# Layer 0's first projection in the order v, RG-LRU, k, q, S5, gates; S5 tables on VectorE held until k is evacuated; S5's end states written later

## The chip, the core and the metric

The kernel runs on one core of a Trainium2 chip. TensorE (PE) multiplies matrices into PSUM, VectorE (DVE), ScalarE (ACT) and GpSimd (POOL) do the elementwise work, and SyncE (SP) issues the DMAs. The metric is the device time of one execution in microseconds.

## The reference, cut to what matters

Two layers run over a prompt of 512 frames and eight running streams of 16 frames each. A layer adds to x the output projection of three mixers side by side, then a squared-ReLU MLP:

```python
hn = _rms_norm(x, p['norm1'])
proj = hn @ p['w_in']                       # u_a, g_a, u_b, q, k, v
out_a = rglru(u_a, g_a)                     # conv of 4, gates, scan, times gelu(g_a)
out_b = s5(u_b)                             # complex scan; z = gelu(y + d*u); z * sigmoid(z @ w_glu + b_glu)
out_c = window_attention(rope(q), rope(k), v, sinks)
x = x + concat(out_a, out_b, out_c) @ w_out
x = x + square(relu(_rms_norm(x, p['norm2']) @ w_up)) @ w_down
```

The outputs are x after both layers and a last norm, and the new states: the last three inputs of the convolution, the last RG-LRU state, the last complex S5 state, and the last keys and values. S5's discretised matrices (A, B, C and powers of A) are computed from the weights inside the kernel.

## The kernel before, in words

All is float32. The 640 columns (512 prompt and 128 sample frames) are cut into two groups g = 0 and 1 of 256 prompt and 64 sample columns, so a matmul moves 320 columns. Activations lie with features on the partitions.

Each projection is a list of `Unit`s. A unit makes 128 output features of one group: 8 slices of 128 input features, in two halves of 4, into one of three PSUM banks of the tag `mm`. `stream` runs units and yields after each half. In the first layer's `in_proj` the weights are used as float32 (line 271, operands `raw` for the first half of a unit and `wl` for the second). Other units split their weights into a high part on ACT (L243, `wh<-raw`) and a rest on DVE (L244, `wl<-raw,wh`), and then take three matmuls for each slice (L274 to L276).

`in_proj` has 12 units: `ua` and `ub` (two each, inputs of RG-LRU and S5), `k`, `v`, four `q`, and two gates `ga`. Their numbers 0 to 11 are in this order, and a unit's output has to be read out of its bank (evacuated) before the third unit after it can start. Evacuations multiply by the norm's factor r: `v` by one DVE operation (L692); `k` and `q` by four ACT copies to `sw` (L705, L706), a POOL product with sin*r (L707) and DVE products with cos*r (L716 for k, L710 for q); `ua` and `ub` of layer 0, group 0, by ACT copies that need no r (L675, L676, L670), with the product by r on POOL later. r comes from the squares (ACT L382, POOL L389, with one buffer `sq` between them, and a last sum on DVE, L386), from sums on PE (L395), a reciprocal root on DVE (L414 to L421), a broadcast on PE (L432) and a copy on ACT (L434). `cs` holds the rope's cos and sin; POOL multiplies both by r (L741).

The first layer's set-up runs at the same time: `s5_small` (DVE operations of 128x32, lines 450 to 536) makes A and its factors, and `layer_small` starts `s5_const`, whose complex products `cmul` (lines 541 to 547, 128x256 each) make the B tables on DVE and the C tables on POOL.

After the first units come the mixers. `mixers` yields after each step of RG-LRU, S5 and attention, and `weave` puts halves of the stream F (the rest of this `in_proj`, then the other group's) between them. The order on PE is the order of the program. The orders on ACT, DVE, POOL and SP are made by a list scheduler, with a model of the time and priorities (`high_priority` for evacuations), so that an edit in one place can move instructions in others. Every engine runs its own list in order. The main program is:

```python
turns(A, 2)
...
small = layer_small(0, P)
next(small)
first(1)
turns(A, 10)
M = mixers(0, P, 0, q[0], m[0], setup[0])
F = chain(A, stream(in_proj(0, 1, norms[1], q[1])))
weave(M, tw[0:9], F, 9)
run(small)
weave(M, tw[9:], F, 19)
```

`first(1)` loads x of group 1 and issues its squares. The mixers of group 1 follow, woven with what is left of F, the output projection of group 0 and its MLP.

Of the kernel before, what the change touches and what calls it, by code (L numbers as in the profile page):

```python
# [11 lines left out]
F32 = mybir.dt.float32  # L12
# [135 lines left out]
def encoder_kernel(ctx: ExitStack, tc: tile.TileContext, a, o):  # L148
# [516 lines left out]
    def in_evac(L, P, g, q, kind, i, pt):  # L665
        r = q.r
        in_alloc(q, *{"ua": ("uap",), "k": ("kS",), "v": ("vS",), "q": ("q", "qS")}.get(kind, (kind,)))
        early = q.early[kind] if kind in q.early else 0
        if kind == "ub" and i < early:
            act(q.ub[:, i], pt, AF.Copy)  # L670
            G.tensor_tensor(q.ub[:, i], q.ub[:, i], r, OP.mult)
        elif kind == "ua" and i < early:
            u = q.uap[:, i]
            v = u[:, 259:335].rearrange("p (b t) -> p b t", t=19)[:, :, 3:19]
            act(u[:, 3:259], pt[:, 0:256], AF.Copy)  # L675
            act(v, pt[:, 256:320].rearrange("p (b t) -> p b t", t=16), AF.Copy)  # L676
            G.tensor_tensor(u[:, 3:259], u[:, 3:259], r[:, 0:256], OP.mult)
            G.tensor_tensor(v, v, r[:, 256:320].rearrange("p (b t) -> p b t", t=16), OP.mult)
        elif kind == "ua":
            u = q.uap[:, i]  # L680
            tt(u[:, 3:259], pt[:, 0:256], r[:, 0:256], OP.mult)
            tt(u[:, 259:335].rearrange("p (b t) -> p b t", t=19)[:, :, 3:19],
               pt[:, 256:320].rearrange("p (b t) -> p b t", t=16), r[:, 256:320].rearrange("p (b t) -> p b t", t=16), OP.mult)
        elif kind == "ub":
            tt(q.ub[:, i], pt, r, OP.mult)
        elif kind == "ga":
            t = tp.tile([128, NG], F32, tag="t", name="t", bufs=2)
            tt(t, pt, r, OP.mult)
            gelu2(V, q.ga[:, i], t)
        elif kind == "v":  # L690
            vT = tp.tile([128, NG], F32, tag="t", name="t", bufs=2)
            tt(vT, pt, r, OP.mult)  # L692
            gcopy(q.vS, vT[:, 256:320])

            def turn():
                b = bank3("sm", 2, 128)
                for j in range(2):
                    transpose(b[:, j], vT[:, 128 * j:128 * j + 128])
                act(kvs[L]["vt"][:, 2 * g:2 * g + 2], b, AF.Copy)

            return turn
        else:
            sw = tp.tile([128, NG], F32, tag="sw", name="sw", bufs=2)
            for p in range(0, 128, 64):
                act(sw[p:p + 32], pt[p + 32:p + 64], AF.Copy)  # L705
                act(sw[p + 32:p + 64], pt[p:p + 32], AF.Copy)  # L706
            G.tensor_tensor(sw, sw, q.sinr, OP.mult)  # L707
            if kind == "q":
                t = tp.tile([128, NG], F32, tag="t", name="t", bufs=2)
                tt(t, pt, q.cosr, OP.mult)  # L710
                tt(q.q[:, i], t[:, 0:256], sw[:, 0:256], OP.add)
                v4 = lambda z: z[:, 256:320].rearrange("p (b t) -> p b t", t=16)
                tt(q.qS[:, :, i], v4(t), v4(sw), OP.add)
            else:
                t = tp.tile([128, NG], F32, tag="t", name="t", bufs=2)
                tt(t, pt, q.cosr, OP.mult)  # L716
                tt(kvs[L]["kT"][:, 256 * g:256 * g + 256], t[:, 0:256], sw[:, 0:256], OP.add)
                tt(q.kS, t[:, 256:320], sw[:, 256:320], OP.add)

    kvs = {}  # L720

    def in_proj(L, g, norm, q, raws=None):

        w_in = a["w_in"][L]
        units = [("ua", 0), ("ua", 1), ("ub", 0), ("ub", 1), ("k", 0), ("v", 0)]
        units += [("q", i) for i in range(4)] + [("ga", 0), ("ga", 1)]
        order = (4, 5, 6, 7, 8, 9, 0, 1, 2, 3, 10, 11) if L == 0 and g == 0 else range(12)

        def begin():
            if g == 0:  # L730
                kvs[L] = {"kT": cst.tile([128, 512], F32, tag="kT", name="kT"), "vt": cst.tile([128, 4, 128], F32, tag="vt", name="vt")}
            q.early = {"ua": 2, "ub": 2} if L == 0 and g == 0 else {"ua": 2}

        def factors():
            norm.finish()
            q.r = norm.r
            cs = tp.tile([128, 2, NG], F32, tag="cs", name="cs", bufs=1)
            q.cosr, q.sinr = cs[:, 0], cs[:, 1]
            dma(cs, a["rope"][g])
            for t in (q.cosr, q.sinr):  # L740
                G.tensor_tensor(t, t, q.r, OP.mult)  # L741

        def evac(kind, i):
            def f(pt):
                with tc.high_priority():
                    return in_evac(L, None, g, q, kind, i, pt)

            return f

        items = [Unit(w_in[n], [(lambda: norm.h, evac(*units[n]))], norm, norm.full, raws if n == order[0] else None) for n in order]  # L750
        items[1].mid, items[2].mid = norm.flush, factors
        return [begin] + items
# [59 lines left out]
    def s5(L, P, g, q, mix, c):  # L812
# [69 lines left out]
        for ct, gs in cts:  # L882
# [5 lines left out]
            n4 = lambda t: t.rearrange("p (n t) -> p n t", t=4)  # L888
            V.scalar_tensor_tensor(n4(zz[:, ct]), n4(u[:, ct]), col("ssm_d", 2 * L + ct), b.rearrange("p t n -> p n t"), OP.mult, OP.add)
            gelu2(V, zz[:, ct], zz[:, ct])  # L890

        sl = D[:, :, 63:80:4]
        for h in range(2):
# [5 lines left out]
        G.tensor_tensor(e, e, bl, OP.add)  # L899
        gcopy(P["send"][:, 128:144], e[:, :, 0])  # L900
        gcopy(P["send"][:, 64 * g:64 * g + 64].rearrange("p (b g) -> p g b", b=4), e[:, :, 1:5])
        sg = c.at(1280, 2, NG)
        yield
        for ct in range(2):
            b = bank("sm")[:, 0:NG]
            for k in range(2):
                mm(b, lhsT=P["wglu"][:, k, 128 * ct:128 * ct + 128], rhs=zz[:, k], start=k == 0, stop=k == 1)  # L907
            act(sg[:, ct], b, AF.Tanh, scale=0.25, bias=hcols[:, 8 + 2 * L + ct:9 + 2 * L + ct])
        V.scalar_tensor_tensor(sg, sg, 1.0, zz, OP.add, OP.mult)
        mix = mix()  # L910
        act(mix[:, 2:4, 0], sg, AF.Copy, scale=0.25)
        V.scalar_tensor_tensor(mix[:, 2:4, 1], sg, 0.25, mix[:, 2:4, 0].bitcast(F32), OP.mult, OP.subtract)
        if g == 1:
            dma(o["send"][L], P["send"])

# [212 lines left out]
        evac = lambda k: lambda pt: out_tile(L, g, k, pt, hm[g])  # L1128
        return [begin] + [Unit(a["w_out"][L, k], [(lambda: mix["mix"](0), evac(k))]) for k in range(8)]

    mark = {}

    def up_evac(norm, am, f, pt):
        t = tp.tile([128, NG], F32, tag="t", name="t", bufs=2)
        V.scalar_tensor_tensor(t, pt, 0.0, norm.r, OP.max, OP.mult)  # L1135
# [33 lines left out]
    def first(g):  # L1169
        norms[g] = Norm(g, n1(0), full=True)  # L1170
        raws = []
        for k in range(0, 8, 2):
            dma(xT[:, g, k:k + 2], a["x"][g, :, k:k + 2])
            if g == 0 and k < 4:
                raws.append(wload(a["w_in"][0, 4], k // 2))
        for k in range(8):
            norms[g].add(k)
        return raws
# [28 lines left out]
    small_prep()  # L1207
    s5_small(lru_const())
    small = layer_small(0, P)
    next(small)  # L1210
    first(1)
    turns(A, 10)
    M = mixers(0, P, 0, q[0], m[0], setup[0])
    tw = WEIGHTS[True]
    F = chain(A, stream(in_proj(0, 1, norms[1], q[1])))
# [72 lines left out]
```

## Time and profile before

| quantity | value |
|---|---|
| median of 3 runs | 1442.09 us (1441.71 to 1443.01) |
| profiled execution, its own time | 1444.44 us |
| its span, first to last instruction | 1442.7 us |
| PE busy | 1384.6 us, 96% |
| DVE, ACT, POOL busy | 857.1, 631.6, 355.5 us |
| PE busy from 330 to 700 us | 368.96 of 370 us |
| PE busy from 190 to 250 us | 52.26 of 60 us |

PE is busy nearly all the time, so the time is the sum of its work, of the waits on PE, and of the stretches in which its granted clock was at the lower of its two levels. A busy share of another engine says little by itself: what counts is whether PE waited for it.

### The profile page before, as it was taken

What the parts mean: (1) busy time and instruction counts of PE and PEld (TensorE: products, weight loads), DVE (VectorE), ACT (ScalarE), POOL (GpSimd) and SP (SyncE); (2) the same over time, 40 slices, a digit from 0 to 9 for tenths busy, and PEclk for the clock granted to TensorE, in tenths of its full rate; (3) what the DMA queues carried; (4) which work ended last, traced back from release to release, by engine and by line L of the source; (5) the groups of instructions that cost most, each with busy time, mean ns of one, the idle gap of its engine ahead of it and who ended that gap; (6) DMA issues with size and microseconds to landing.
All of it is one profiled execution on the core that took longest, in us unless ns stands there. A gap on an engine that the chain in (4) does not pass through costs nothing.

```text
span 1442.7 us, 25209 instructions
## 1 busy us (share of the span) xinstructions
PE 1384.6 (96%) x9390; PEld 1303.2 (90%) x9390; DVE 857.1 (59%) x1702; ACT 631.6 (44%) x1315; POOL 355.5 (25%) x575
## 2 busy tenths in 40 slices
PE   8897989999999999999989998999999999999997
PEld 6565678899999999999988897889999999999997
DVE  7677278766644344446687768775664434434574
ACT  3344475545432123135675667654543312313543
POOL 4546053601014007001244225420100100100111
PEclk8899999999999999999989999999999999999998
DMA  6221223244422222234423342333442222223452
GB/s 236 77 78 65 87 90 127 89 159 142 152 90 80 75 74 67 78 108 149 132 91 105 112 148 75 125 105 118 147 147 95 74 80 75 80 75 109 148 176 95
DMA packets 91387, 156.24 MB, mean 108 GB/s; under 512 B 14336, under 2 KB 18304, under 8 KB 91264
## 3 DMA queue, kind: packets, MB, share of 16 engines
q1 hardware_dynamic: 91264, 154.63, 32.2%
q8 instruction: 74, 1.21, 0.3%
q14 instruction: 49, 0.40, 0.1%
HBM read 151.02 MB, written 3.37 MB: 107 GB/s over the span
## 4 chain that ended last, share of the span: by engine, by line
PE 80%; DVE 6%; POOL 5%; ACT 3%; issue 2%; DVEq 0%; POOLq 0%; ACTq 0%
PE mm L274 24%; PE mm L276 23%; PE mm L275 23%; PE mm L271 3%; PE sm L176 1%; PE sm L1045 1%; DVE wl L244 1%; DVE bigf L861 1%; PE sm L1024 1%; PE sm L879 1%; PE sm L907 1%; PE fin L432 1%; DVE bigf L864 0%; DVE bigf L866 0%; PE fin L395 0%
## 5 line engine op out<-in xcount | busy, mean ns | idle before, releaser
L276 PE MATMUL mm<-bigr,wl 128*128 128x320 f32 x2496 | 777.4, 311 | 18.4 <-DVE wl L244 18.4
L274 PE MATMUL mm<-bigr,wh 128*128 128x320 f32 x2496 | 785.5, 315 | 2.4 <-POOL bigr L156 1.9
L275 PE MATMUL mm<-bigr,wh 128*128 128x320 f32 x2496 | 775.2, 311 | 1.7 <-DVE bigr L1138 1.6
L243 ACT ACTIVATE wh<-raw 128x512 fp32r<-128x512 f32 x496 | 312.0, 631 | 482.8 <-PE mm L275 462.7
L276 PEld LDWEIGHTS mm<-bigr,wl 128*128 128x128 f32 x2496 | 472.2, 189 | 23.1 <-DVE wl L244 22.5
L274 PEld LDWEIGHTS mm<-bigr,wh 128*128 128x128 f32 x2496 | 472.3, 189 | 13.5 <-issue 6.8
L275 PEld LDWEIGHTS mm<-bigr,wh 128*128 128x128 f32 x2496 | 472.6, 189 | 3.0 <-DVE bigr L1138 2.4
L244 DVE TENSOR_TENSOR wl<-raw,wh 128x512 fp32r<-128x512 f32 x496 | 352.9, 712 | 171.4 <-ACT wh L243 161.2
L156 POOL TENSOR_SCALAR bigr<-t 128x320 fp32r<-128x320 f32 x128 | 61.9, 485 | 613.2 <-ACT t L1136 612.5
L1120 DVE TENSOR_TENSOR xT<-xT,mm 128x320 f32<-128x320 f32 x160 | 77.8, 486 | 128.4 <-PE mm L276 128.0
L1138 DVE TENSOR_TENSOR bigr<-t,bigr 128x320 fp32r<-128x320 f32 x128 | 70.6, 551 | 73.4 <-POOL bigr L156 73.3
L1136 ACT ACTIVATE t<-t 128x320 f32<-128x320 f32 x128 | 60.1, 472 | 122.3 <-DVE t L1135 103.0
L1135 DVE SCALAR_TENSOR_TENSOR t<-mm,r 128x320 f32<-128x320 f32 x128 | 62.3, 489 | 77.0 <-PE mm L276 76.3
L389 POOL TENSOR_TENSOR ss<-ss,sq 128x320 f32<-128x320 f32 x52 | 50.9, 979 | 202.9 <-ACT sq L382 202.9
L271 PE MATMUL mm<-bigf,raw 128*128 128x320 f32 x200 | 64.9, 473 | 9.6 <-issue 9.5
L271 PEld LDWEIGHTS mm<-bigf,raw 128*128 128x128 f32 x200 | 40.4, 208 | 28.2 <-issue 15.5
L271 PE MATMUL mm<-bigf,wl 128*128 128x320 f32 x184 | 56.9, 454 | 0.0
L271 PEld LDWEIGHTS mm<-bigf,wl 128*128 128x128 f32 x184 | 35.4, 199 | 14.3 <-issue 2.3
L364 ACT ACTIVATE bigr<-xT,sm 128x320 fp32r<-128x320 f32 x48 | 27.0, 562 | 17.1 <-DVE xT L1120 16.3
L707 POOL TENSOR_TENSOR sw<-sw,cs 128x320 f32<-128x320 f32 x20 | 20.1, 1005 | 55.7 <-ACT sw L706 48.5
L365 DVE SCALAR_TENSOR_TENSOR bigr<-xT,sm,bigr 128x320 fp32r<-128x320 f32 x48 | 30.6, 637 | 0.1
L382 ACT ACTIVATE sq<-xT 128x320 f32<-128x320 f32 x59 | 27.2, 460 | 5.6 <-POOL ss L389 4.8
(296 smaller groups left out, 1081.5 us busy)
## 6 DMA issues: line engine op xcount, KB each, us to landing
raw<-w_up SPq DMA_DIRECT2D x192, 256.0 KB, 2.6
raw<-w_down SPq DMA_DIRECT2D x192, 256.0 KB, 2.6
raw<-w_in SPq DMA_DIRECT2D x73, 256.0 KB, 2.6
raw<-w_out SPq DMA_DIRECT2D x64, 256.0 KB, 2.6
wl<-w_in SPq DMA_DIRECT2D x23, 256.0 KB, 2.6
xT<-x SPq DMA_DIRECT2D x8, 320.0 KB, 6.1
yT<-xT SPq DMA_DIRECT2D x8, 320.0 KB, 3.7
cs<-rope SPq DMA_DIRECT2D x4, 320.0 KB, 3.3
```

What stands on the lines that cost most here:

```text
L156: return G.tensor_scalar(out, in_, 1.0, 0.0, OP.mult, OP.add)
L243: act(h, raw, AF.Copy)
L244: tt(l, raw, h.bitcast(F32), OP.subtract)
L271: mm(pt, lhsT=self.w[n][:, k % 4], rhs=m[:, k], start=k == 0, stop=k == 7)
L274: mm(pt, lhsT=h[:, k % 4], rhs=m[:, k, 0], start=k == 0, stop=False)
L275: mm(pt, lhsT=h[:, k % 4], rhs=m[:, k, 1], start=False, stop=False)
L276: mm(pt, lhsT=l[:, k % 4], rhs=m[:, k, 0], start=False, stop=k == 7)
L389: G.tensor_tensor(self.ss, self.ss, sq, OP.add)
L1120: tt(xT[:, g, k], xT[:, g, k], pt, OP.add)
L1135: V.scalar_tensor_tensor(t, pt, 0.0, norm.r, OP.max, OP.mult)
L1136: act(t, t, AF.Square)
L1138: mark["dve"] = tt(am[:, f, 1], t, am[:, f, 0].bitcast(F32), OP.subtract)
```

## The change

It has five parts: (1) layer 0's first projection runs as v, ua, ua, k, q, q, q, q, ub, ub, ga, ga instead of k, v, q, q, q, q, ua, ua, ub, ub, ga, ga, and 16 halves instead of 12 are issued ahead of the mixers; (2) `next(small)` comes after ten halves instead of two, and its DVE instructions (not those of POOL or SP) may not be placed ahead of k's evacuation L716; (3) the products cs*r get high priority; (4) S5's end states (`je`, `e`) stand after the GLU in the program text; (5) the first loads are those of v.

```diff
-                tt(t, pt, q.cosr, OP.mult)
+                mark["k"] = tt(t, pt, q.cosr, OP.mult)
...
-        order = (4, 5, 6, 7, 8, 9, 0, 1, 2, 3, 10, 11) if L == 0 and g == 0 else range(12)
+        order = (5, 0, 1, 4, 6, 7, 8, 9, 2, 3, 10, 11) if L == 0 and g == 0 else range(12)
...
-            for t in (q.cosr, q.sinr):
-                G.tensor_tensor(t, t, q.r, OP.mult)
+            with tc.high_priority():
+                for t in (q.cosr, q.sinr):
+                    G.tensor_tensor(t, t, q.r, OP.mult)
...
-        sl = D[:, :, 63:80:4]
-        for h in range(2):
-            act(je[64 * h:64 * h + 64], sl[64 - 64 * h:128 - 64 * h], AF.Copy)
...
         sg = c.at(1280, 2, NG)
         yield
...
+        sl = D[:, :, 63:80:4]
+        for h in range(2):
+            act(je[64 * h:64 * h + 64], sl[64 - 64 * h:128 - 64 * h], AF.Copy)
...
-                raws.append(wload(a["w_in"][0, 4], k // 2))
+                raws.append(wload(a["w_in"][0, 5], k // 2))
...
     small = layer_small(0, P)
-    next(small)
+    turns(A, 8)
+    with tc.issue_after(mark["k"].ins):
+        next(small)
     first(1)
-    turns(A, 10)
+    turns(A, 6)
```

The lines of the changed kernel are one lower or one higher than before in some places (L741 becomes L742, L858 becomes L859, L865 becomes L866). On DVE, at the evacuations of v (L692) and k (L716) in the first projection, the kernel before has, with `tab` the S5 tables and `s5s` S5's small values:

```order
L533 TENSOR_TENSOR bigf<-bigf 128x32
L541 TENSOR_TENSOR tab<-s5s,tab 128x256
L546 TENSOR_TENSOR tab<-s5s,tab 128x256
L534 TENSOR_TENSOR s5s<-bigf 128x32
L543 TENSOR_TENSOR tab<-tab 128x16x16
L716 TENSOR_TENSOR t<-mm,cs 128x320
L692 TENSOR_TENSOR t<-mm,r 128x320
L535 TENSOR_TENSOR s5s<-s5s 128x32
```

and the changed one:

```order
L531 COPY s5s<-bigf 128x32
L532 SCALAR_TENSOR_TENSOR s5s<-bigf,sgn 128x32
L533 TENSOR_TENSOR bigf<-bigf 128x32
L534 TENSOR_TENSOR s5s<-bigf 128x32
L386 SCALAR_TENSOR_TENSOR ss<-ss,sq 128x320
L535 TENSOR_TENSOR s5s<-s5s 128x32
L536 SCALAR_TENSOR_TENSOR s5s<-s5s 128x32
L692 TENSOR_TENSOR t<-mm,r 128x320
L716 TENSOR_TENSOR t<-mm,cs 128x320
L541 TENSOR_TENSOR tab<-s5s,tab 128x256
```

All ten table products (128x256) that stood ahead of the two evacuations are now behind them; all the 128x32 operations of `s5_small` stand ahead of them still, with L386 between.

On POOL, in the first group's S5 mixer (products L858, L859 and L865), the kernel before has:

```order
L858 TENSOR_TENSOR bigf<-bigf,tab 128x8x79
L852 MEMSET bigf 128x16
L859 TENSOR_TENSOR bigf<-bigf 128x8x79
L677 TENSOR_TENSOR uap<-uap,r 128x256 x2
L678 TENSOR_TENSOR uap<-uap,r 128x4x16 x2
L741 TENSOR_TENSOR cs<-cs,r 128x320 x2
L156 TENSOR_SCALAR bigf<-sm 128x4x8
L156 TENSOR_SCALAR coll<-uap 128x3
L865 TENSOR_TENSOR bigf<-bigf,tab 128x640
```

and the changed one:

```order
L742 TENSOR_TENSOR cs<-cs,r 128x320 x2
L677 TENSOR_TENSOR uap<-uap,r 128x256 x2
L678 TENSOR_TENSOR uap<-uap,r 128x4x16 x2
L975 TENSOR_SCALAR att<-att,st_998 128x192 x2
L804 TENSOR_TENSOR bigf<-bigf,ga 128x2x64
...
L859 TENSOR_TENSOR bigf<-bigf,tab 128x8x79
L860 TENSOR_TENSOR bigf<-bigf 128x8x79
...
L866 TENSOR_TENSOR bigf<-bigf,tab 128x640
```

The six products with the second group's r moved from between S5's second and third product to the front of all of them. (Four more copies L156 stand where the first "..." is, and L156, the second L859 and L860 and two memsets where the second is.)

On ACT, in the gelu of the first group's S5 (L650 and L652, with `gw` its tile), the kernel before has:

```order
L650 ACTIVATE gw<-bigf 128x320
L652 ACTIVATE gw<-gw 128x320
L705 ACTIVATE sw<-mm 32x320
L706 ACTIVATE sw<-mm 32x320
L705 ACTIVATE sw<-mm 32x320
L706 ACTIVATE sw<-mm 32x320
L650 ACTIVATE gw<-bigf 128x320
L652 ACTIVATE gw<-gw 128x320
```

and the changed one:

```order
L650 ACTIVATE gw<-bigf 128x320
L243 ACTIVATE wh<-raw 128x512
L652 ACTIVATE gw<-gw 128x320
L705 ACTIVATE sw<-mm 32x320
...
L650 ACTIVATE gw<-bigf 128x320
L243 ACTIVATE wh<-raw 128x512
L652 ACTIVATE gw<-gw 128x320
```

Two weight copies of the output projection moved between the two halves of each gelu. On PE, four halves of `in_proj` fewer stand between the first group's mixers' end and the start of the output projection; the S5 end states of part (4) stay where they were in the built order (right behind S5's last product).

## Rows read from the trace of the kernel before

**Rows 1.** Waits of PE from 0 to 250 us: total, times, longest.

```profile
PE mm L271 <- issue: 9.5, 1, 9.5
PE mm L276 <- DVE wl L244: 7.5, 6, 2.1
PE sm L1045 <- ACT att L1036: 5.4, 1, 5.4
PE sm L1045 <- ACT att L964: 4.1, 1, 4.1
...
PE sm L907 <- DVE bigf L653: 0.9, 1, 0.9
```

**Rows 2.** Windows: length, busy us (count) of PE, PEld, DVE, ACT, POOL, PEclk, DMA share, GB/s.

```profile
31.70:41.20 9.50, 0.00 (x0) 0.03 (x1) 9.43 (x26) 1.71 (x4) 6.20 (x9) 0.77 0.08 28
41.20:47.00 5.80, 5.80 (x12) 3.83 (x13) 5.76 (x16) 0.38 (x1) 5.41 (x6) 0.50 0.06 13
112.00:115.00 3.00, 3.00 (x6) 2.01 (x7) 2.96 (x7) 0.75 (x4) 2.02 (x4) 0.50 0.00 0
143.50:149.40 5.90, 5.90 (x16) 3.29 (x16) 0.99 (x3) 0.38 (x1) 0.79 (x2) 0.50 0.34 97
```

**Rows 3.** Timeline of PE: start, busy, instruction, idle before it and its releaser.

```profile
41.20 4.60 PE L271 MATMUL mm<-bigf,raw 128*128 128x320 f32 x8 [9.53 <-issue]
```

**Rows 4.** Timeline of DVE, 27 to 42 us.

```profile
27.80 0.92 DVE L386 SCALAR_TENSOR_TENSOR ss<-ss,sq 128x320 f32<-128x320 f32 x1
28.64 0.59 DVE L511 TENSOR_SCALAR s5s<-bigf,sgn 128x32 f32<-128x32 f32 x1
...
39.41 0.18 DVE L533 TENSOR_TENSOR bigf<-bigf 128x32 f32<-128x32 f32 x1
...
40.62 0.48 DVE L716 TENSOR_TENSOR t<-mm,cs 128x320 f32<-128x320 f32 x1
41.02 0.48 DVE L692 TENSOR_TENSOR t<-mm,r 128x320 f32<-128x320 f32 x1
```

**Rows 5.** Windows of DVE alone, instructions that touch `tab`: length, busy (count), PEclk, DMA.

```profile
30.86:40.62 9.76, 5.49 (x10) 0.80 0.08 27
```

**Rows 6.** Windows, all engines, as rows 2.

```profile
28.60:38.00 9.40, 3.07 (x14) 1.90 (x12) 9.26 (x21) 2.15 (x5) 9.02 (x12) 0.93 0.18 56
```

**Rows 7.** Timeline of ACT: the copy that makes r.

```profile
29.36 0.44 ACT L434 ACTIVATE r<-fin 128x320 f32<-128x320 f32 x1 [2.69 <-DVE bigf L518]
```

**Rows 8.** Timeline of POOL: end of the first busy stretch; S5 of group 0.

```profile
36.94 1.03 POOL L707 TENSOR_TENSOR sw<-sw,cs 128x320 f32<-128x320 f32 x1
...
127.06 2.42 POOL L677 TENSOR_TENSOR uap<-uap,r 128x256 f32<-128x256 f32 x2
...
129.98 2.26 POOL L741 TENSOR_TENSOR cs<-cs,r 128x320 f32<-128x320 f32 x2
```

**Rows 9.** Timeline of PE in the first group's mixers: two long waits, and a float32 half.

```profile
111.25 0.65 PE L1045 MATMUL sm<-att,vt 128*64 128x256 f32 x4 [4.08 <-ACT att L964]
...
143.47 1.98 PE L1045 MATMUL sm<-att,vt 128*64 128x256 f32 x8 [5.37 <-ACT att L1036]
...
155.84 2.37 PE L271 MATMUL mm<-bigf,raw 128*128 128x320 f32 x8
```

**Rows 10.** Timeline of ACT, 160 to 180 us: a half of the gelu, the first weight copies.

```profile
160.14 0.47 ACT L652 ACTIVATE gw<-gw 128x320 f32<-128x320 f32 x1 [0.56 <-DVE gw L651]
...
173.66 0.63 ACT L243 ACTIVATE wh<-raw 128x512 fp32r<-128x512 f32 x1 [2.93 <-DMA raw<-w_out]
```

**Rows 11.** DMA issues of SP: DMA, queue, count, KB each, us to landing.

```profile
raw<-w_out SPq DMA_DIRECT2D x64, 256.0 KB, 2.6
```

**Rows 12.** Windows of the second group's mixers, as rows 2.

```profile
190.00:250.00 60.00, 52.26 (x395) 47.47 (x394) 51.41 (x92) 37.33 (x87) 30.98 (x42) 0.97 0.31 104
```

More of the change, by code (lines that the diff above doesn't have):

```diff
@@ L715, in in_evac @@
                 t = tp.tile([128, NG], F32, tag="t", name="t", bufs=2)
-                tt(t, pt, q.cosr, OP.mult)
+                mark["k"] = tt(t, pt, q.cosr, OP.mult)
                 tt(kvs[L]["kT"][:, 256 * g:256 * g + 256], t[:, 0:256], sw[:, 0:256], OP.add)
                 tt(q.kS, t[:, 256:320], sw[:, 256:320], OP.add)
-    kvs = {}
+    kvs, mark = {}, {}
     def in_proj(L, g, norm, q, raws=None):
@@ L890, in s5 @@
             gelu2(V, zz[:, ct], zz[:, ct])
-        sl = D[:, :, 63:80:4]
-        for h in range(2):
-            act(je[64 * h:64 * h + 64], sl[64 - 64 * h:128 - 64 * h], AF.Copy)
-        lay = lambda t: t[:, 16 * L:16 * L + 16].unsqueeze(2).to_broadcast([128, 16, 5])
-        G.tensor_tensor(e, sl, lay(A4R), OP.mult)
-        G.tensor_tensor(je, je, lay(A4I), OP.mult)
-        G.tensor_tensor(e, e, je, OP.add)
-        G.tensor_tensor(e, e, bl, OP.add)
-        gcopy(P["send"][:, 128:144], e[:, :, 0])
-        gcopy(P["send"][:, 64 * g:64 * g + 64].rearrange("p (b g) -> p g b", b=4), e[:, :, 1:5])
         sg = c.at(1280, 2, NG)
@@ L912, in s5 @@
         V.scalar_tensor_tensor(mix[:, 2:4, 1], sg, 0.25, mix[:, 2:4, 0].bitcast(F32), OP.mult, OP.subtract)
+        sl = D[:, :, 63:80:4]
+        for h in range(2):
+            act(je[64 * h:64 * h + 64], sl[64 - 64 * h:128 - 64 * h], AF.Copy)
+        lay = lambda t: t[:, 16 * L:16 * L + 16].unsqueeze(2).to_broadcast([128, 16, 5])
+        G.tensor_tensor(e, sl, lay(A4R), OP.mult)
+        G.tensor_tensor(je, je, lay(A4I), OP.mult)
+        G.tensor_tensor(e, e, je, OP.add)
+        G.tensor_tensor(e, e, bl, OP.add)
+        gcopy(P["send"][:, 128:144], e[:, :, 0])
+        gcopy(P["send"][:, 64 * g:64 * g + 64].rearrange("p (b g) -> p g b", b=4), e[:, :, 1:5])
         if g == 1:
@@ L1129, in out_proj @@
         return [begin] + [Unit(a["w_out"][L, k], [(lambda: mix["mix"](0), evac(k))]) for k in range(8)]
-    mark = {}
     def up_evac(norm, am, f, pt):
```

## The prediction

> **What bounds the kernel now.** I read the busy shares first (PE is busy 96% of the span), so only waits of PE and its low clock can be won back. The waits of PE up to 250 us [rows 1] come next: later PE is nearly full, and the change leaves the second layer's order as it was. The reader is to see three big ones: 9.5 us once at L271, 5.4 and 4.1 us at L1045 in the first group's mixers; then 7.5 us in six pieces for the split weights of L276. Then the clock in windows [rows 2]: it is at its lower level (0.50, that is 1.2 of 2.4 GHz) for 5.8 us behind the first wait, for 3.0 behind the 4.1 one, for 5.9 behind the 5.4 one. Work at half the clock costs half of such a stretch more, so 2.9, 1.5 and 2.95 us.
>
> Last, what the first wait is for. The profile calls it "issue", without a releaser. PE stops at 41.20 - 9.53 = 31.67 [rows 3], when three units fill the three banks; the fourth needs the bank of the first, k, and PE goes on 0.1 us behind the end of k's last read, L716 at 40.62 + 0.48 [rows 4]. So it is k's evacuation. DVE is full in the wait, 9.43 of 9.50 us [rows 2], and ten products of S5's tables take 5.49 us of it [rows 5]. r had been there since 29.36 + 0.44 [rows 7].
>
> **The change part by part: the first wait.** v is now first and needs only r and one DVE operation, L692; both units of ua are freed by ACT copies. The ten table products leave the front of it. What stays in front of L692, in one list, are 22 operations of 128x32 from L511 on, L386 and two more: 25. When do they end?
>
> From below: the trace's L692 began at 41.02; less 5.49 for the products, less 0.40 for L716 that now comes behind, plus 0.2 for the two that came ahead gives 35.3. PE then goes on at 35.3 + 0.48 + 0.1 = 35.9, a gain of 5.3.
>
> From above: while POOL was busy, DVE got 21 operations done in 9.40 us, 0.45 each, against 12 of POOL [rows 6]. Such an operation shows 0.18 us at 39.41, where POOL is idle, and 0.59 at 28.64, where it is not [rows 4]. POOL has thirteen operations between the start of its C tables and the copy of v, as it had before, so it is busy to about 37.97 again [rows 8]. 25 operations at 0.45 from 27.80 on (where L386 stood) end at 39.0; PE goes on at 39.6, a gain of 1.6.
>
> The products that leave were themselves partly waiting for POOL, and this waiting falls to whatever is next in DVE's list. So I stand nearer to the upper bound: L692 begins at 37.3, PE goes on at 37.9, gain **3.3**. The new wait is then 6.2 us, longer than the 5.37 us behind which the clock was low for 5.9 us [rows 2, 9]: the clock costs what it did, nothing gained.
>
> The Trainium skill, in "SBUF — State Buffer", section "SBUF: two separate sides", says that GpSimd and certain VectorE operations share a port pair that is locked for a whole instruction, and the other side waits. By that rule alone DVE would keep the pace of the mixed stretch, the gain would be 1.6, and the whole sum 1.7 us smaller; by subtraction alone it would be 2.0 larger. The trace agrees as to the kind of wait (0.59 against 0.18 us), and doesn't say how many operations slip through between two of POOL's.
>
> **Two units more ahead of the mixers** bring four halves of float32 matmuls forward; that is work moved, not removed, and costs nothing by itself. The gates' gelu leaves the stretch in which DVE makes S5's decay tables, but the second group's rsqrt comes in: I count nothing for both.
>
> **POOL in S5.** In the trace L677, L678 and L741 of the second group hold POOL from 127.06 to 129.98 + 2.26 = 132.24, so 5.2 us [rows 8], between S5's second and third product, and on the way to the 5.4 us wait (143.47) [rows 9]. They now go ahead of the first product. There they are hidden so far as POOL waits for ACT's copies of S5's inputs, and push the products by the rest. I take 1.5 for the rest (bounds 0 and 5.2): gain **3.7**.
>
> **The clock behind that wait.** If the wait shrinks from 5.4 towards 4, its low stretch shrinks from 5.9 towards 3.0 us, up to 1.5 us less. I take **1.0** (0 to 1.5).
>
> **Weight copies ahead of the gelu.** The L243 that now stands between L650 and L652 waits for a load of `w_out`, whose buffer comes free only when PE has read a float32 half; since the output projection starts four halves earlier, that is the half just ahead of the gelu. The load takes 2.6 us [rows 11], and ACT waited 2.93 us for the first one before too, where nobody was behind it [rows 10]. The gelu's first step ends some 1.5 us behind that half (an estimate: before, the float32 half that began at 155.84 ended at 158.21 [rows 9], S5's transposes follow it, and the first L652 began at 160.14 [rows 10], 1.9 later, of which 0.4 is a DVE step behind L650), so L652 comes 2.9 - 1.5 = 1.4 late plus 0.63 for the copy; of the four L705 and L706 behind it the second half hides a part. PE's wait at L907, 0.9 [rows 1], grows to 2.8: **-1.9** (0 to -5, if both copies wait in full).
>
> **Four halves of the output projection more among the second group's mixers**, in place of four that need no splitting. There DVE is busy 51.41 of 60 us [rows 12] and PE waits 7.5 us for L244 already [rows 1]. Four more L243 are 2.5 us of ACT [rows 10], as much again on DVE. Most fall before 190 us, where DVE has room: **-1.0** (0 to -2.5). The end states of S5 don't move in the built order: nothing.
>
> **Sum**: 3.3 + 3.7 + 1.0 - 1.9 - 1.0 = 5.1 us. From the profiled execution's own 1444.44 this gives 1439.3; that execution lies 2.35 above the median 1442.09, from which it gives **1437.0**.
>
> **The rivals.**
> *A, DVE runs free.* The small operations, without the tables between them, slip through POOL's gaps, and L692 ends by 33.5 or so. For it: the stretches at 39.4, with 0.18 us each [rows 4]. Against it: POOL is busy there now, and was not at 39.4. The first wait falls to 2 us, the clock doesn't drop behind it (the three waits with a low window behind them are of 4.08 us and more [rows 2, 3, 9]), and the gain there is 8 + 2.9 instead of 3.3: 1429.4.
>
> *B, it moves waits only.* L692 keeps the upper bound (1.6), and POOL's products ahead of S5 push all behind them by their full 5.2 us, so that nothing is gained at 143.47, nor in the clock. 1.6 - 1.9 - 1.0 = -1.3: 1443.4. For it: POOL's work isn't less, and S5 comes at the end of it either way. Against it: POOL waits for ACT just ahead of S5's first product, in which time products can run.
>
> *C, the other side: the tables' loads come late.* `next(small)` is issued later, so the loads of S5's B and C stand behind five of the first projection's on SP's queue. DVE's first use of them stands in its list ahead of the reciprocal root of r and of all 25 operations. Side by side, five loads cost little more than one, 2.6 us; one behind another, 13 us [rows 11]. Some 3 of it are hidden by other operations of `s5_small` that now go first (an estimate: some 28 at 0.1), the rest delays r and L692 alike. It decides from a delay of 3.3 + 1.8 + 2.9 = 8 us on (the gain there, the rest of the sum, the bound below); at 10 us the time is 1437.0 + 10 = 1447. For it: SP's list runs in order, and waits of one load hold the next. Against it: the buffers of the first loads are free from the start, so nothing but the queue holds them apart.
>
> **How the numbers follow.** Forecast 0.48 (1433.5 to 1440), A 0.20, B 0.23, C 0.09. Less than 0.2%, 2.9 us, can't be told from no change. Of the forecast's cases nine in ten lie below 1439.2, and A's all: faster 0.65. B's mostly, and the rest of the forecast, are the same: 0.24. C, and a few of B with a fuller weight wait: slower 0.11. The range goes from A's 1429 to B's 1443.5, which leaves out C and the better half of A's spread.
>
> **What would show it.** Right: PE idle at L271 of about 6 us, ending some 0.1 behind L692; small DVE operations of 0.4 to 0.8 us ahead of it; clock 0.50 behind it; the wait at the mixers' second L1045 (L1046 now) some 3 to 4 us; a wait of 2 to 3 us at the GLU's matmuls, with L243 on DMA ahead of L652. Wrong: L692 before 35 (A); S5's first product more than 3 us later behind the mixers' first long wait than it was (B); DVE waiting for the tables' load at L579 (C). Beyond these, waits for L244 of much over 7.5 us in the second group's mixers would say that the weights' term was too small.

## The result, and the profile after

| | before | after |
|---|---|---|
| median, runs side by side | 1442.55 us (1441.71 to 1444.29, 4 runs) | 1453.20 us (1450.70 to 1454.03, 4 runs) |
| profiled execution, its own time | 1444.44 us | 1454.03 us |
| its span | 1442.7 us | 1452.2 us |
| PE, DVE, ACT, POOL busy | 1384.6, 857.1, 631.6, 355.5 us | 1384.0, 864.1, 632.9, 354.4 us |

The changed kernel is slower: ratio 1.0067, 95% interval 1.0052 to 1.0082, some 10.6 us. The forecast was 1437.0. PE's busy time is the same, so the loss is time in which PE stands still: 68.2 us of the span in place of 58.1. The waits of PE in the changed kernel, 0 to 330 us (total, times, longest), answer to [rows 1]:

```profile
PE sm L1046 <- ACT att L1037: 7.2, 1, 7.2
PE mm L276 <- DVE wl L244: 6.9, 6, 1.9
PE sm L176 <- DVE t L692: 5.6, 1, 5.6
PE sm L982 <- DVE qS L713: 4.8, 1, 4.8
PE sm L1046 <- ACT att L965: 4.4, 1, 4.4
PE fin L432 <- DVE rsq L421: 2.8, 2, 1.9
PE sm L897 <- DVE bigf L653: 2.3, 1, 2.3
...
PE mm L275 <- DVE bigr L365: 2.2, 2, 2.0
PE mm L274 <- ACT bigr L364: 2.1, 1, 2.1
PE mm L271 <- DVE t L710: 1.0, 1, 1.0
```

The first wait did shrink, from 9.5 to 5.6 us. But the wait at the mixers' second L1046 grew from 5.4 to 7.2 where it was to shrink; there is a new one of 4.8 for q (L713), the one at the GLU grew from 0.9 to 2.3 (L897, before L907), and L364 and L365 are new (the norm's copies for the MLP, they end between 242.9 and 246.4 us).

The windows of the changed kernel answer to [rows 2] (length, busy us of PE, PEld, DVE, ACT, POOL, clock, DMA share, GB/s):

```profile
27.50:36.00 8.50, 5.07 (x20) 3.26 (x19) 8.26 (x16) 1.66 (x5) 8.42 (x13) 1.00 0.18 62
36.20:37.60 1.40, 0.00 (x0) 0.00 (x0) 1.33 (x11) 0.00 (x0) 0.00 (x0) 0.50 0.00 0
...
38.10:43.00 4.90, 4.87 (x11) 3.35 (x12) 0.00 (x0) 0.38 (x1) 3.80 (x11) 0.52 0.04 8
...
156.00:162.50 6.50, 6.50 (x18) 3.58 (x18) 0.99 (x3) 0.38 (x1) 0.40 (x2) 0.52 0.28 83
179.10:182.40 3.30, 3.30 (x7) 2.12 (x8) 0.00 (x0) 1.00 (x2) 0.00 (x0) 0.53 0.00 0
```

Two things are to be seen. From 38.10 to 43.00 DVE does nothing at all, in the very stretch in which it made tables before. And the clock is at its lower level behind the 5.6 us wait, behind the 7.2 one, and behind the 2.3 one at the GLU as well. (It is at 0.50 behind the 4.8, the 4.4 and the L364 and L365 waits too, from 68.91 to 73.40, from 122.36 to 128.00 and from 244.20 to 250.90.)

DVE in the changed kernel around the first evacuations answers to [rows 4]:

```profile
37.59 0.48 DVE L692 TENSOR_TENSOR t<-mm,r 128x320 f32<-128x320 f32 x1
44.87 0.49 DVE L716 TENSOR_TENSOR t<-mm,cs 128x320 f32<-128x320 f32 x1 [6.79 <-ACT sw L706]
45.27 0.73 DVE L541 TENSOR_TENSOR tab<-s5s,tab 128x256 f32<-128x256 f32 x1
```

PE in the same stretch ([rows 3]):

```profile
30.25 2.32 PE L271 MATMUL mm<-bigf,raw 128*128 128x320 f32 x8
38.13 0.69 PE L176 MATMUL sm<-ident,t 128*128 128x128 f32 x2 [5.56 <-DVE t L692]
38.62 4.38 PE L271 MATMUL mm<-bigf,wl 128*128 128x320 f32 x8
...
68.91 2.19 PE L982 MATMUL sm<-att,qS 64*64 64x144 f32 x16 [4.80 <-DVE qS L713]
```

L692 begins at 37.59. L716, the anchor of the hold, comes next on DVE, but it reads the fourth unit: that unit's second half runs at the low clock up to 43.00, and four ACT copies follow. So all of DVE's table work stands still for 6.79 us, and from 45.27 on lies between the evacuations of q, which PE then waits for at 68.91.

S5 of the first group, DVE and then POOL of the changed kernel (POOL answers to [rows 8]):

```profile
134.69 3.91 DVE L771 SCALAR_TENSOR_TENSOR bigf<-uap,sm,bigf 128x332 f32<-128x332 f32 x4
138.52 0.48 DVE L851 TENSOR_TENSOR bigf<-sm,tab 128x316 f32<-128x316 f32 x1
138.92 1.03 DVE L771 SCALAR_TENSOR_TENSOR bigf<-uap,sm,bigf 128x332 f32<-128x332 f32 x2
139.87 0.48 DVE L851 TENSOR_TENSOR bigf<-sm,tab 128x316 f32<-128x316 f32 x1
140.56 4.35 DVE L862 TENSOR_TENSOR_SCAN bigf<-tab,bigf 128x640 f32<-128x640 f32 x2 [0.22 <-POOL bigf L853]
```

```profile
123.50 1.68 POOL L742 TENSOR_TENSOR cs<-cs,r 128x320 f32<-128x320 f32 x2
125.14 1.28 POOL L677 TENSOR_TENSOR uap<-uap,r 128x256 f32<-128x256 f32 x2
...
132.37 1.32 POOL L859 TENSOR_TENSOR bigf<-bigf,tab 128x632 f32<-128x632 f32 x1 [2.65 <-ACT bigf L850]
```

POOL's products for the second group are gone from between S5's products, as forecast, and POOL waits for ACT ahead of the first one. But since those products are done early, the second group's convolution (L771) is ready early too, and takes 4.9 us of DVE in front of S5's products L851 and its scans L862.

ACT of the changed kernel, at S5's last step and the gelu ([rows 10]):

```profile
152.74 0.69 ACT L906 ACTIVATE sj<-bigf 64x80 f32<-64x80 f32 x2 [4.10 <-DVE bigf L867]
...
155.23 0.60 ACT L1037 ACTIVATE att<-sm 128x512 f32<-128x512 f32 x1
...
173.60 0.63 ACT L243 ACTIVATE wh<-raw 128x512 fp32r<-128x512 f32 x1 [1.19 <-DMA raw<-w_out]
174.13 0.46 ACT L652 ACTIVATE gw<-gw 128x320 f32<-128x320 f32 x1
...
177.51 0.63 ACT L243 ACTIVATE wh<-raw 128x512 fp32r<-128x512 f32 x1 [0.66 <-DMA raw<-w_out]
178.05 0.45 ACT L652 ACTIVATE gw<-gw 128x320 f32<-128x320 f32 x1
```

L1037, for which PE waits 7.2 us, stands behind a copy that waits for S5's last subtraction L867. Both halves of the gelu's L652 stand behind a weight copy that waits for its load.

### The profile page after: what moved, and what is told of

Read it like the earlier page. It is cut to its first block, busy times and chain, and to the rows that moved or that the text cites. A ratio compares the mean times of both kernels' runs of the same rounds, so it can differ in the third digit from the quotient of the medians.

```text
span 1452.2 us, 25217 instructions
## 1 busy us (share of the span) xinstructions
PE 1384.0 (95%) x9390; PEld 1301.0 (90%) x9390; DVE 864.1 (60%) x1702; ACT 632.9 (44%) x1315; POOL 354.4 (24%) x575
## 4 chain that ended last, share of the span: by engine, by line
PE 80%; DVE 10%; ACT 3%; issue 3%; POOL 2%; DMA 1%; SPq 0%; DVEq 0%; ACTq 0%; POOLq 0%
PE mm L274 23%; PE mm L276 23%; PE mm L275 23%; PE mm L271 3%; PE sm L176 1%; DVE wl L244 1%; PE sm L1046 1%; PE sm L880 1%; PE sm L1025 1%; DVE bigf L862 1%; PE sm L897 1%; DVE bigf L771 1%; DVE bigf L867 0%; PE fin L432 0%; PE sm L1000 0%
## 5 line engine op out<-in xcount | busy, mean ns | idle before, releaser
L276 PE MATMUL mm<-bigr,wl 128*128 128x320 f32 x2496 | 776.0, 311 | 17.2 <-DVE wl L244 17.2
L243 ACT ACTIVATE wh<-raw 128x512 fp32r<-128x512 f32 x496 | 312.2, 632 | 487.7 <-PE mm L275 466.2
L244 DVE TENSOR_TENSOR wl<-raw,wh 128x512 fp32r<-128x512 f32 x496 | 356.7, 720 | 169.5 <-ACT wh L243 158.0
L156 POOL TENSOR_SCALAR bigr<-t 128x320 fp32r<-128x320 f32 x128 | 62.5, 490 | 610.2 <-ACT t L1135 609.4
L271 PEld LDWEIGHTS mm<-bigf,raw 128*128 128x128 f32 x200 | 39.3, 202 | 19.5 <-issue 4.3
L364 ACT ACTIVATE bigr<-xT,sm 128x320 fp32r<-128x320 f32 x48 | 27.0, 563 | 21.7 <-DVE xT L1121 20.9
L975 POOL TENSOR_SCALAR att<-att,st 128x192 f32<-128x192 f32 (+2 forms) x24 | 20.6, 866 | 34.8 <-ACT wh L243 22.2
```

Source lines behind the costliest of these rows:

```text
L156: return G.tensor_scalar(out, in_, 1.0, 0.0, OP.mult, OP.add)
L243: act(h, raw, AF.Copy)
L244: tt(l, raw, h.bitcast(F32), OP.subtract)
L271: mm(pt, lhsT=self.w[n][:, k % 4], rhs=m[:, k], start=k == 0, stop=k == 7)
L276: mm(pt, lhsT=l[:, k % 4], rhs=m[:, k, 0], start=False, stop=k == 7)
```

## The experiments

Times are given as the difference to the kernel before, run on the same chip beside it; the changed kernel is at +10.65. Line numbers shift by some lines where an edit adds any.

**1 and 2: the hold.** The first hangs the tables on v's evacuation (the first unit), the second on nothing, with `next(small)` still after ten halves.

```diff
-            tt(vT, pt, r, OP.mult)
+            mark["v"] = tt(vT, pt, r, OP.mult)
...
-    with tc.issue_after(mark["k"].ins):
+    with tc.issue_after(mark["v"].ins):
         next(small)
```

```diff
-    with tc.issue_after(mark["k"].ins):
-        next(small)
+    next(small)
```

> The changed kernel, with S5's table products on VectorE held behind v's evacuation (L692) instead of k's (L716); nothing else moves on PE or ACT. Theory (the hold behind k leaves VectorE idle for 6.8 us while PE makes k, and the tables then stand among the evacuations of q, where PE waits 1.0 and 4.8 us): the wait ahead of L692 stays at 5.6 us; VectorE works through 38 to 45 us; PE's waits on L710 and L713 fall from 5.8 to under 1.5 us; the time is 5 to 8 us below the changed kernel, so 1445 to 1448 (1.002 to 1.004 of before). Rival (the loss comes from 16 instead of 12 halves ahead of the mixers): no more than 2 us, 1451 or above.

> The changed kernel without the hold: seven of the table products stand ahead of L692 again. Theory: PE's wait for L692 grows from 5.6 by about 2 to 3 us, VectorE's idle time at k goes, the waits on L710 and L713 fall from 5.8 to under 2; the time is 2 to 5 us below the changed kernel, 1448 to 1451. Rival (the hold does its work, the loss is elsewhere): 2 to 3 us above the changed kernel, 1455 to 1456.

Measured: behind v 1447.1, **+3.9** (ratio 1.0030, 1.0019 to 1.0041); without a hold 1448.1, **+4.9** (1.0034, 1.0021 to 1.0047). Both lie in the range of the theory. The wait at L982 falls from 4.8 to 2.1 (expected: under 1.5 with L710) and 1.0 us; the wait for L692 is 5.2 and 6.7. So the hold behind k costs some 6 us, and one that ends 7 us sooner can't be told from none. (The early wait for r at L432, 1.95 us in the changed kernel's profile and not in these two, explains little of it: L432 begins at 26.99 there and in run 1 alike, since PE came to it sooner, with 3.4 us of low clock ahead of it in place of 6.8.)

**3 and 4: the convolution, the weight copies.** On the changed kernel, once the second group's L771 are held on DVE behind the first group's last S5 subtraction, once the first four weight copies of `w_out` are held on ACT behind the second half of S5's gelu.

```diff
-            tt(d, d, jz, OP.subtract)
+            mark["s5", L, g] = tt(d, d, jz, OP.subtract)
...
-            for j in range(1, 4):
-                V.scalar_tensor_tensor(xc, u[:, ct, j:j + LP], col("conv_w", 8 * L + 2 * j + ct), xc, OP.mult, OP.add)
+            with tc.issue_after(mark["s5", 0, 0].ins) if (L, g) == (0, 1) else nullcontext():
+                for j in range(1, 4):
+                    V.scalar_tensor_tensor(xc, u[:, ct, j:j + LP], col("conv_w", 8 * L + 2 * j + ct), xc, OP.mult, OP.add)
```

```diff
-            act(h, raw, AF.Copy)
+            with tc.issue_after(hold.ins) if hold is not None else nullcontext():
+                act(h, raw, AF.Copy)
...
             gelu2(V, zz[:, ct], zz[:, ct])
+            mark["glu", L, g] = mark["tanh"]
...
-        return [begin] + [Unit(a["w_out"][L, k], [(lambda: mix["mix"](0), evac(k))]) for k in range(8)]
+        return [begin] + [Unit(a["w_out"][L, k], [(lambda: mix["mix"](0), evac(k))], hold=mark["glu", L, g] if (L, g) == (0, 0) and k < 2 else None) for k in range(8)]
```

(`mark["tanh"]` is the gelu's last ACT step, L652.)

> The changed kernel, with the second group's convolution (six L771 on VectorE, 4.9 us) held behind the last subtraction of the first group's S5 (L867); PE and ACT keep their order. Theory (the products with r came earlier on GpSimd, so the convolution came earlier on VectorE, ahead of S5's scans): the wait of 7.2 us at the mixers' second L1046 falls to 3 to 4.5, and the time by 2.5 to 4 us, to 1449 to 1451. Rival (the chain through ACT's copies sets that wait): under 1 us, 1452 to 1454.

> The changed kernel, with the first four weight copies of the output projection (L243) held behind the second half of S5's gelu on ACT. Theory (they wait for a load between the two halves of the gelu): PE's wait of 2.3 us at the GLU falls to about 1, and the low clock behind it goes (1.6 us): 2.5 to 3.5 us less, 1449.5 to 1451. Rival (PE then waits for the split weights at the output projection's start instead): no change, 1452 to 1454.

Measured: convolution later 1450.39, **+7.2** (1.0060, 1.0044 to 1.0077), the second long wait 4.0 in place of 7.2 us; weight copies later 1448.78, **+5.6** (1.0043, 1.0028 to 1.0058), the wait at the GLU 1.3 in place of 2.3, with the clock not low behind it. The first theory holds; so does the second as to the place, but it gains more than its 2.5 to 3.5 us: in the profiles 3.3 us lie between the second group's L432 and the MLP's norm, as expected, but 1.8 ahead of that L432 (112.18 in place of 113.94), where run 4 edits nothing. With the convolution held, DVE runs the scans first:

```profile
136.86 4.42 DVE L863 TENSOR_TENSOR_SCAN bigf<-tab,bigf 128x640 f32<-128x640 f32 x2 [0.97 <-POOL bigf L854]
...
148.60 1.13 DVE L772 SCALAR_TENSOR_TENSOR bigf<-uap,sm,bigf 128x332 f32<-128x332 f32 x2
```

**5, 6 and 7: more behind v, and all together.** The fifth is the first, with the last 26 small operations of `s5_small` behind v as well. The sixth is 1 + 3 + 4, the seventh 5 + 3 + 4.

```diff
-    s5_small(lru_const())
+    tail = s5_small(lru_const())
+    next(tail)
...
+    with tc.issue_after(mark["v"].ins):
+        run(tail)
+        next(small)
```

> The kernel of e1, with the last part of s5_small (26 operations of 128x32 from the squares for den on) held behind v's evacuation too. Theory (L692 waits for VectorE's list, which GpSimd's products slow down): L692 runs at about 32 us, the wait ahead of v's transposes falls from 5.2 us to under 1.5, the clock stays up behind it; 3 to 5 us less than e1 (1447.1), so 1442 to 1444. Rival (VectorE's work only moves on to the evacuations of q, as it did in the change): the wait at L982 grows from 2.1 to 5 or more, under 1.5 us less than e1, 1445.6 or above.

> e1, e3 and e4 together. Theory (three separate waits): their gains add up, 1453.2 - 6.1 - 2.8 - 4.4 = 1440, between 1438.5 and 1442. Rival (one chain, whose waits only change places): 1444 or above.

> e5, e3 and e4 together: by the theory 3 to 5 us below e6, 1435 to 1438, and faster than the kernel before by 0.3 to 0.5 per cent; by the rival of e5 no less than 1439.

Measured: 1447.8, **+4.8** (1.0036, 1.0023 to 1.0049); 1440.82, **-2.1** (0.9988, 0.9979 to 0.9998); 1439.48, **-3.5** (0.9983, 0.9966 to 0.9999). In the fifth L692 ends at 32.87, PE's wait for it is gone, and the time is not better than the first's, as the rival has it. The wait has moved to the next evacuation; PE of the fifth:

```profile
47.38 4.00 PE L271 MATMUL mm<-bigf,raw 128*128 128x320 f32 x8 [2.83 <-DVE t L717]
63.00 1.20 PE L983 MATMUL sm<-att,qS 64*64 64x144 f32 x16 [2.35 <-DVE qS L714]
```

The three edits of the sixth together give 12.8 us against the changed kernel; one by one they gave 6.7, 3.4 and 5.0, which is 15.1. The sixth lies where its theory has it. The seventh has the lowest median, but its runs go from 1438.48 to 1444.51, so that it can't be told from the sixth; its interval ends just below 1, and its time is the one that the rival of run 5 gives.

**8: fewer woven halves.** 48 in place of 52 halves are woven among the second group's mixers.

```diff
-        weave(M, tw, F, 58 if L else 52)
+        weave(M, tw, F, 58 if L else 48)
```

> The changed kernel, with 48 instead of 52 halves woven into the second group's mixers of layer 0, as many as there were of the output projection and the MLP before. Theory (four halves more of split weights there make VectorE and ACT late for the MLP's first input): PE's waits for L364 and L365 (4.3 us from 240 to 247 us) go, 2 to 4 us less than the changed kernel, 1449 to 1451. Rival (the waits come from the mixers' own chain): within 1 us, 1452 to 1454.

Measured: 1459.94, **+17.0** (1.0115, 1.0100 to 1.0130), 6.3 worse than the changed kernel. My theory fell: the waits at L364 and L365 only shrink from 4.3 to 2.8 us, and PE's longest wait of that stretch is now 5.45:

```profile
233.91 0.64 PE L276 MATMUL mm<-bigr,wl 128*128 128x320 f32 x1 [5.45 <-DVE wl L244]
```

From the second group's L432 to the next norm's PE does the same 1486 instructions in the eighth (first row) and in the changed kernel:

```profile
111.99:368.67 256.68, 228.35 (x1486) 194.68 (x1487) 167.64 (x298) 131.74 (x292) 90.33 (x124) 0.93 0.32 100
113.94:364.30 250.36, 224.66 (x1486) 192.30 (x1487) 166.57 (x298) 131.66 (x292) 90.94 (x124) 0.95 0.32 103
```

This stretch is 6.3 us longer, as much as the medians are apart: 2.6 of it is standing still (28.3 for 25.7), 3.7 is more time for the same work, with the clock at 0.50 behind the long wait (234.00 to 238.50) and again later. So the halves there are cover: without four of them PE waits longer at a time and runs at the low clock behind it.

**9, 10 and 11: one part at a time.** The ninth is the kernel before with 16 halves ahead of the mixers, the tenth the kernel before with the later `next(small)` and the hold behind k, k still first. The eleventh has the order and the 16 halves of the change, without the rest.

```diff
-    turns(A, 10)
+    turns(A, 14)
```

```diff
-    next(small)
+    turns(A, 8)
+    with tc.issue_after(mark["k"].ins):
+        next(small)
     first(1)
-    turns(A, 10)
+    turns(A, 2)
```

and on the changed kernel, beside the product with cs and the end states put back:

```diff
-    turns(A, 8)
-    with tc.issue_after(mark["k"].ins):
-        next(small)
+    next(small)
     first(1)
-    turns(A, 6)
+    turns(A, 14)
```

> The kernel before with one number changed: 16 halves ahead of the mixers where it has 12 (k, v, four q, ua, ua), everything else as it was, the early next(small) and the order k first included. It does the fourth and fifth part of the woven work alone. The prediction's step (work moved, not removed, costs nothing by itself; one microsecond for the weights): 1442 to 1444. The theory now (each half that is taken from the second group's mixers is cover that is missing there, about 1.7 us apiece, and the output projection that stands in its place reaches the first group's gelu with its weight copies): PE's waits behind 150 us grow as in the changed kernel, 1447 to 1450, with a wait of about 2 us at the GLU's matmuls and waits of some 4 us at L364 and L365.

> The kernel before, k first and 12 halves ahead of the mixers as it was, with the second part of the change alone: next(small) after ten halves, and none of its DVE instructions ahead of k's L716. It asks whether the hold does what the prediction wanted of it where k is the first unit. Theory (a hold behind a unit that is evacuated first makes no gap, since DVE is late with L716 anyway): L716 begins at about 37, the first wait falls from 9.5 to about 6, DVE has no idle stretch behind it, and the tables delay q's evacuations by 1 to 3 us; 1440 to 1443. Rival (the tables behind any evacuation cost what they gave, because they are 30 us of DVE that has to lie somewhere ahead of S5): 1443 to 1446, with waits of PE on L710 or L713 as long as what the first wait lost.

> The changed kernel with parts 2, 3 and 4 undone: order v, ua, ua, k, q and 16 halves remain, next(small) is early as in the kernel before, and nothing is held. If the prediction was right that the ten table products stand in front of the first evacuation and have to go, L692 begins at about 40 to 41 as k's product did before, the first wait of PE is about 9 us, and the time is about 3 above that of the changed kernel without the hold, 1450 to 1452. Rival (the ACT evacuations of ua keep PE busy, and tables that are made early are out of the way of q's evacuations): the first wait is long but nothing follows it, 1446 to 1449.

Measured: 16 halves alone 1451.34, **+7.6** (1.0060, 1.0047 to 1.0073); the hold alone 1443.43, **-0.3** (0.9996, 0.9987 to 1.0005); order and halves 1449.47, **+5.8** (1.0040, 1.0028 to 1.0052). The ninth is a little slower than even the theory had it, and its waits are those of the changed kernel from the mixers on:

```profile
PE mm L271 <- issue: 10.6, 1, 10.6
PE sm L1045 <- ACT att L1036: 7.2, 1, 7.2
...
PE sm L1045 <- ACT att L964: 4.4, 1, 4.4
PE sm L907 <- DVE bigf L653: 2.4, 1, 2.4
...
PE mm L275 <- DVE bigr L365: 2.2, 2, 2.0
PE mm L274 <- ACT bigr L364: 2.1, 1, 2.1
```

The tenth can't be told from the kernel before, as its rival has it. DVE shows what the hold does where k is first: L716 begins at 37.38 in place of 40.62 [rows 4].

```profile
37.38 0.48 DVE L716 TENSOR_TENSOR t<-mm,cs 128x320 f32<-128x320 f32 x1
...
38.18 0.41 DVE L541 TENSOR_TENSOR tab<-s5s,tab 128x256 f32<-128x256 f32 x1
```

And PE shows where it goes: 3.24 us sooner at the fourth unit (before: 41.20), but 3.00 us of wait at q (before: 0.87), which ends 0.10 behind q's last evacuation L713, with the clock at 0.50 behind it (58.80 to 62.00), so that L981 ends only 1.2 us sooner (before: 60.91 and 1.20 long).

```profile
37.96 4.22 PE L271 MATMUL mm<-bigf,raw 128*128 128x320 f32 x8 [7.51 <-issue]
58.76 2.19 PE L981 MATMUL sm<-att,qS 64*64 64x144 f32 x16 [3.00 <-issue]
```

For the eleventh both expectations missed a part. DVE makes tables ahead of L692, yet L692 begins at 38.88, only 1.3 us later than in the changed kernel without them; the wait is 6.7 us and not 9. In time it lies between the two.

```profile
38.54 0.41 DVE L547 TENSOR_TENSOR tab<-tab 128x256 f32<-128x256 f32 x1
38.88 0.48 DVE L692 TENSOR_TENSOR t<-mm,r 128x320 f32<-128x320 f32 x1
```

**12: the ninth with the two edits of 3 and 4.**

> The kernel before with 16 halves ahead of the mixers (which alone gave 1451.3, +7.6) and the two edits that were tried on the changed kernel: the second group's convolution products L771 behind the first group's last S5 subtraction on DVE, and the first four weight copies of w_out behind the second half of S5's gelu on ACT. Theory (what the four early halves cost is that the second group's work and the output projection's weight copies reach the first group's S5 and gelu four halves sooner and stand in front of it): the two edits give back 2.8 and 4.4 as they did there, 1444 to 1445, with the second L1045 wait at about 4 us, the clock of the stretch behind it nearer to full, and the GLU wait at about 1.3. Rival (the loss is that four float32 halves are missing as cover in the second group's mixers, where split halves stand in their place and wait for DVE): no more than 2 to 3 us come back, 1448 to 1449.5, and the W waits of L244, L364 and L365 stay as they are and make up the rest.

Measured: 1446.89, **+4.3** (1.0027, 1.0017 to 1.0038): 3.3 of the 7.6 come back, between the two expectations. The second L1045 wait is 4.0 and the one at the GLU 1.3 us, as the theory has it. The waits at L364 and L365 stay (1.8 and 2.1), as the rival has it. The two profiled executions can't say where the other 4.3 us lie: they are only 0.6 us apart (1445.05, the fastest of run 12, and 1444.44, one of the longer ones of the kernel before).

## Why the prediction was wrong

The runs take the change apart:

| step | us |
|---|---|
| 16 halves ahead of the mixers in place of 12 (run 9) | +7.6 |
| the order v, ua, ua, k, q (run 11 less run 9) | -1.9 |
| `next(small)` later without a hold, cs*r sooner, end states later in the text (run 2 less run 11) | -0.8 |
| the hold behind k (the changed kernel less run 2) | +5.7 |
| sum | +10.6 |

The rows are differences of neighbours, so they add up to the whole by construction. Each run's interval is some 2 us to either side: +7.6 and +5.7 are clear of it, -1.9 and -0.8 can't be told from nothing.

The prediction had 3.3 us of gain for the order and the hold together, where the last three rows are a loss of 3.0, and 1.8 for all that follows from the 16 halves (3.7 + 1.0 - 1.9 - 1.0), where the first row is a loss of 7.6.

**The step that failed first: "Two units more ahead of the mixers ... that is work moved, not removed, and costs nothing by itself."** It cost 7.6 us. What the four halves move is not only their own work: everything in F behind them comes four halves sooner against the first group's mixers, and so do its demands on DVE and ACT. Runs 3, 4 and 12 show two of these demands: the convolution ahead of S5's scans, the weight copies ahead of the gelu, 3.3 us of the 7.6. The other 4.3 isn't settled. The waits at L364 and L365, which only kernels with 16 halves show, are of that size (4.3 us in run 9, 3.9 in run 12), but no run took them away by themselves, and up to the MLP's norm PE stands still only 1.4 us longer in run 12's profile, with them, than in that of the kernel before (33.7 us up to 242.01, 32.2 up to 240.33). The second group's rsqrt, for which I counted nothing, is a wait of 0.8 us at L432 (run 9, at 112.28).

**POOL in S5, +3.7, had the wrong sign.** Its first half held: the products are hidden, and S5's first product comes 10.0 us behind the first long wait's end (122.36 to 132.37), in the kernel before 9.5 (111.25 to 120.78). So rival B's sign isn't there. But I followed POOL alone. The products release the convolution, which DVE then runs first. From the first product to ACT's first copy of a scan's result (L864, before L863) it is now 11.1 us (to 143.44), before 7.8 (120.78 to 128.55). The rest of S5 makes up for most of that; its last subtraction, before and after:

```profile
139.49 0.81 DVE L866 TENSOR_TENSOR bigf<-bigf 128x640 f32<-128x640 f32 x1
...
151.90 0.81 DVE L867 TENSOR_TENSOR bigf<-bigf 128x640 f32<-128x640 f32 x1
```

It ends 19.5 us behind the first product before, 20.3 after: 0.8 us lost in place of 3.7 won. In run 3, where the convolution stands behind it, it ends 17.2 us behind (131.51 to 148.68), 2.4 sooner than before, and the wait is 4.0, as the forecast of 3 to 4 had it. So POOL's part of the mechanism was right, at 2.4 of its 3.7 us; the convolution on DVE took it away. With that **the clock behind it, +1.0,** fell too: 6.5 us at 0.52, before 5.9 at 0.50 [rows 2].

**"The ten table products leave the front of it": right where they left, never asked where they land.** L692 begins at 37.59, forecast 37.3; PE goes on 0.06 us behind its end; the clock is low behind it. That term is right to 0.3 us, and run 10 shows the same step for k (3.24 us, forecast 3.3); the bounds were worked out, the place between them was a judgement, so a part of this nearness is luck. But the hold names k, and I took k's evacuation to follow at once, since in the kernel before both stand side by side [rows 4]. In the new order k is three units later, so DVE stands idle 6.8 us, and the tables go among q's evacuations. Run 1 gives 6.7 us back by moving the anchor. Run 10 says more: even without a gap, 2.1 of the 3.2 us that the first wait gives are taken at q, and the rest doesn't show in the time. The tables are work that DVE has to do ahead of S5; with them behind one evacuation, the next ones come later.

**"The fourth needs the bank of the first."** In the new order it doesn't, though the text ahead of the prediction says so of every unit: k's first half runs at 30.25, with L692 seven microseconds off (ACT's copies of the first ua had ended at 25.96). PE does one half more and stops at v's transposes, from 32.57 on where it stopped at 31.67 before, so the wait is 5.6 us in place of the forecast 6.2.

**The weight copies, -1.9,** were right in kind and place (L243 on DMA ahead of L652, a GLU wait of 2.3, forecast 2.8). Their price was too small: I didn't expect the clock to drop behind so short a wait, which is 1.5 us more in this profile (L897 takes 3.40 us, and 1.88 in run 11 behind the same wait), and run 4 gives 5.0 back, 3.3 of them in this stretch.

**"Four halves of the output projection more among the second group's mixers", -1.0,** went by a wrong picture. The waits for L244 fell (7.5 to 6.9), and four halves fewer made the kernel slower (run 8): they are cover there. What the term left out are the 4.3 us at L364 and L365 and the low clock behind them; 2.8 of these stay in run 8, so the four halves are not their only cause.

Of the rivals, A's condition was made in run 5 (L692 done by 32.87, no wait): its 11 us weren't there, since DVE had the next evacuation still to do. Its premise that only waits of 4.08 us and more have a low clock behind them overlooked a place in the trace, as the last section shows. C's wait at L579 was 0.2 us, and for no load. I had no rival for a hold that makes an engine idle, and none for work that overtakes on DVE; for that the time lay above the range.

The Trainium skill, in "SBUF — State Buffer", section "SBUF: two separate sides", calls the port pair that VectorE and GpSimd share an exclusive lock. The trace agrees in kind: 16 instructions of DVE in 8.5 us with POOL full, 11 in 1.4 us with POOL idle. No run took POOL's work away. The 1.6 that I worked out for its case and the 5.3 by subtraction lie on either side of the 3.2 that run 10 shows.

## What to carry to other kernels

When an instruction is to wait for another, read when that other one ends in the *new* order, and what the engine has left to do until then. When the order of a filler stream moves by a few pieces, list for each engine what each later piece asks of it and what stands behind that on its list; a piece that comes early is not free where engines run lists in order. A wait that is shortened by putting work behind it counts only once the next reader of that engine has been followed.

## What the runs showed of the hardware that was not expected

The same wait may or may not have the low clock behind it. PE at the GLU of the changed kernel (first row) and of run 11:

```profile
179.08 3.40 PE L897 MATMUL sm<-bigf,gg 128*128 128x320 f32 x6 [2.34 <-DVE bigf L653]
...
173.30 1.88 PE L907 MATMUL sm<-bigf,gg 128*128 128x320 f32 x6 [2.34 <-DVE bigf L653]
```

The clock is at 0.53 from 179.10 to 182.40 in the one and at 1.00 from 173.30 to 176.70 in the other. Behind waits of 2.33 to 2.41 us these matmuls take 3.28 to 3.57 us in the changed kernel and in runs 1, 2, 8 and 9, and 1.88 us in runs 3, 5 and 11. The wait's length alone doesn't decide it; what does is not shown here. The trace of the kernel before had such a place too, which the prediction overlooked, behind a wait of 2.13 us for L244 (PE goes on at 223.45):

```profile
224.50:227.90 3.40, 3.40 (x15) 3.40 (x14) 3.40 (x8) 1.90 (x7) 1.45 (x3) 0.50 0.45 149
```

DVE's small operations beside a busy POOL leave room for larger ones: the seven table products ahead of L692 in run 11 show 5.0 us of busy time and delay it by 1.3 us, and the ten of the kernel before show 5.49 [rows 5] and delay L716 by 3.24 (run 10).
